# Another order for the seven products of a pooled pair, collected in one PSUM tile with ScalarE copies between

## The chip, the core and the metric

The kernel runs on one core of one Trainium2 chip. The metric is the device time of one execution in microseconds (us). Before the change the median of three runs is 782.64 us (782.56 to 784.69).

## What is computed

The reference is a small decoder trunk with two layers, 512 tokens (16 meta tokens are put in front of them and dropped at the end) and a width of 1024. All values are fp32. In each layer one normalised input is projected by one wide matrix, and two token mixers work side by side on slices of the result; each mixer's output is gated by a sigmoid of a slice of its own.

```
h = rmsnorm(h_res, norm_gain[l])
proj = h @ w_in[l]
u_pool, z_pool, c_q, c_kv, k_rope, z_mla, g_pool, g_mla = jnp.split(proj, IN_SPLIT_POINTS, axis=-1)
y_pool = (pool_mix(u_pool, pool_w_group[l], pool_scale[l]) * jax.nn.silu(z_pool)) @ pool_w_up[l]
o_mla = mla(c_q, c_kv, k_rope, pos, ...)
y_mla = (o_mla * jax.nn.silu(z_mla)) @ mla_w_up[l]
merged = jax.nn.sigmoid(g_pool) * y_pool + jax.nn.sigmoid(g_mla) * y_mla
h_res = h_res + merged @ w_out[l]
```

The change concerns only one matrix product: g_pool = h @ (its 1024 columns of w_in), in the last layer.

## The kernel before

**Products in three matmuls.** Activations lie with channels on the 128 partitions and tokens along the free axis. Every fp32 operand is split into a rounded high part and a low part, and a product is the sum of three matmuls, high x high, low x high and high x low (`mm3`, L192, L195, L196). Weights come in chunks of 128 x 512: SP's queue loads a chunk into one of three buffers raw (L115), ScalarE casts it to whi (L187), VectorE subtracts to get wlo (L188); whi and wlo have three buffers each. Chunks are loaded a few products ahead.

**The order of the work.** A list `plan` names the products (a Gemm each) in the order of the program, and the generator `stream()` issues it piece by piece. In the last layer the plan's end runs gm0, gm1, gp0, gm2, gp1, gm3, gp2, gm4, gp3, gm5, gm6, gm7: gm are the tiles of the other gate, gp0 to gp3 the four pairs of g_pool's eight tiles. Attention runs beside it: each head is issued in steps, and between two steps `fill` advances the stream by a fixed number of nanoseconds as the generator counts them. A scheduler in the framework then sets the final order of each engine's instructions; so the order that is run differs in places from the one that is written. The engines PE (TensorE), ACT (ScalarE), DVE (VectorE), POOL (GpSimd) and SP (SyncE, which only issues DMAs) each run their instructions in that order and wait on semaphores.

**Seven products for eight.** In the last layer a pair of g_pool's tiles (256 output channels) is worked out by a Strassen-Winograd scheme: two halves of the input channels (chunks 0 to 3 and 4 to 7 of h) and two halves of the tokens (256 each) make it a 2 x 2 block product, done in seven products in place of eight. Products 1, 2 and 3 take plain tokens; 4, 5, 6 and 7 take sums and differences of token halves that `mixed` (L588) prepares on VectorE as the input is normalised. The sums of weight blocks for 3, 5, 6 and 7 are made in DRAM by accumulating DMAs early on (wsumgp). A product is 12 matmuls of 128 x 256 (four input chunks, three matmuls each). Its result goes to a PSUM tile called mm, of which there are four, shared with all other Gemms.

`fast` (L608 to 654) issues the pair u in the order 1, 6, 7, 5, 2, 4, 3 with four PSUM tiles: a holds 1, onto which 2 is accumulated; b holds 6; c holds 7, onto which 4 is accumulated; d holds 5, onto which 3 is accumulated. After 1, ScalarE copies a to part[u] in SBUF (a slot of the tag sv, L632). VectorE subtracts 6 from it (L634), subtracts that from 7 (L636) and 5 from the result (L638), which is one of the four blocks; 2 lets a second block be read straight from PSUM; after 4 VectorE subtracts (L644), and after 3 it adds (L647). Each finished block goes to `got_gp` (L655): a tanh on ScalarE (L657) and one VectorE operation (L658) that multiplies it into the pooled mixer's output am.

**What stands beside it.** In the stretch of the pairs TensorE also runs the other gate's tiles (mm<-hh,whi, 512 columns), the scores of a head (S<-kh,qhl), transposes of its probabilities (L979, written mm<-cst,pa and mm<-cst,cq), its output (o<-th,vt, L984) and transposes at L990 and L1007. ScalarE casts (th, L303) and takes exponentials (L915). SP's queue also moves rotated keys: kp<-kn (L866) and, when that has landed, kn<-kp (L877), ahead of whatever was queued later. In the output stage behind the gates, a PSUM tile S is emptied by ScalarE (sv<-S, L1163) and used again for the next products; it is named here because the prediction reads some of its rows.

Of the kernel before, what the change touches and what calls it, by code (L numbers as in the profile page):

```python
# [13 lines left out]
AF = mybir.ActivationFunctionType  # L14
# [4 lines left out]
P = 128  # L19
# [3 lines left out]
NM = 16  # L23
T = SEQ + NM
HALF = T // 2
# [14 lines left out]
MT_GP = 16  # L40
# [32 lines left out]
def trunk(ctx, tc, xT, pos, win, wkr, wqb, wkb, wvb, wgr, wpu, wmu, wout, gains, const, yT):  # L73
    nc = tc.nc
    pe, act, dve, gp, sp = nc.tensor, nc.scalar, nc.vector, nc.gpsimd, nc.sync
# [115 lines left out]
    def mm3(out, wh, wl, xh, xl, start, stop, more=False, hold=False):  # L191
        first = pe.matmul(out, wh, xh, start=start, stop=False, skip_group_check=more)  # L192
        if hold:
            behind(first, newest[0])
        pe.matmul(out, wh, xl, start=False, stop=False, skip_group_check=more)  # L195
        newest[0] = pe.matmul(out, wl, xh, start=False, stop=stop, skip_group_check=more)  # L196
        past.append((clk[0], newest[0]))
# [140 lines left out]
    wsum = {n: [dp.tile([P, 4, 512], F32, name=f"wsum{n}{u}") for u in range(k)] for n, k in (("gp", 4), (0, 2), (1, 2))}  # L338
    gate = dp.tile([P, 6, SEQ], F32, name="gate")
# [3 lines left out]
    N2 = SEQ // 2  # L343
    XH = [(NM, NM + N2), (NM + N2, T)]
    (a, b), (_, c) = XH

    def weight_sums(name, w):
# [13 lines left out]
        for u in range(len(w) // 2):  # L361
            for fn, i in ((copy, 0), (copy, 2), (add, 0), (copy, 1), (add, 2), (add, 1), (copy, 3), (add, 3)):
                yield lambda fn=fn, u=u, i=i: fn(*made(u, i))

    class Layer:
        def __init__(self, l):
            self.l, self.last = l, l == DEPTH - 1
# [218 lines left out]
        def mixed(self, i):  # L586
            k, s = divmod(i, 2)
            if k > 3 or not self.last:  # L588
                return
            u, w = self.f[k], self.f[k + 4]  # L590
            if s == 0:
                dve.tensor_sub(w[:, b:c], u[:, b:c], w[:, b:c])
                dve.tensor_sub(u[:, b:c], u[:, a:b], u[:, b:c])
                dve.tensor_sub(u[:, a:b], u[:, a:b], w[:, b:c])
                dve.tensor_sub(w[:, a:b], w[:, a:b], u[:, a:b])
                return
            if k == 0:
# [10 lines left out]
        def fast(self, name, a, b, u, got):  # L608
            order = (1, 6, 7, 5, 2, 4, 3)
            s = wsum["gp"][u]  # L610
            src = {1: a[:, 0:512], 2: a[:, 512:1024], 4: b[:, 512:1024], 5: s[:, 0, :], 6: s[:, 1, :], 7: s[:, 2, :],
                   3: s[:, 3, :]}
            bank = {}

            def body(i, w):
                p = order[i]
                key = {1: "a", 2: "a", 6: "b", 7: "c", 4: "c", 5: "d", 3: "d"}[p]
                if key not in bank:
                    bank[key] = mmt()
                ps = bank[key][:, :N2]  # L620
                t, o = (XH[1] if p == 3 else XH[0]), (0 if p == 1 else 4)
                for k in range(4):
                    xh, xl = (x[:, t[0]:t[1]] for x in self.hs[k + o]) if p < 4 else self.tt[k][p]
                    c = P * k
                    mm3(ps, w[0][:, c:c + P], w[1][:, c:c + P], xh, xl, k == 0 and p not in (2, 4, 3), k == 3, True)
                    if k == 1:
                        yield 6 * (N2 / 2.4)
                if p == 1:
                    self.part[u] = slot("sv", bufs=2)
                d, v = self.part[u][:, 0:N2], self.part[u][:, HALF:HALF + N2]  # L630
                if p == 1:
                    act.activation(d, ps, AF.Copy)  # L632
                elif p == 6:
                    dve.tensor_sub(d, d, ps)  # L634
                elif p == 7:
                    dve.tensor_sub(v, ps, d)  # L636
                elif p == 5:
                    dve.tensor_sub(v, v, ps)  # L638
                    got(2 * u + 1, XH[1], v, v)
                elif p == 2:  # L640
                    got(2 * u, XH[0], ps, tmp()[:, :N2])
                elif p == 4:
                    x = tmp()[:, :N2]
                    dve.tensor_sub(x, ps, d)  # L644
                    got(2 * u + 1, XH[0], x, x)
                else:
                    dve.tensor_add(d, d, ps)  # L647
                    got(2 * u, XH[1], d, d)
                if i == len(order) - 1:
                    done.add((self.l, name))  # L650
                yield 6 * (N2 / 2.4)

            plan.append(Gemm((self.l, name), [src[p] for p in order], 512 * len(order), body=body))

        def got_gp(self, m, s, v, t):  # L655
            am = self.am[m][:, s[0]:s[1]]
            act.activation(t, v, AF.Tanh, scale=0.5)  # L657
            dve.scalar_tensor_tensor(out=am, in0=t, scalar=1.0, in1=am, op0=ALU.add, op1=ALU.mult)  # L658

        def window(self, m):  # L660
            s = self.us[m]
# [551 lines left out]
        def register(self, nxt):  # L1213
            l, XS = self.l, self.XS
            wi = lambda t: win[l, t]
# [49 lines left out]
            if self.last:  # L1265
                for e in ("gm0", "gm1", "gp0", "gm2", "gp1", "gm3", "gp2", "gm4", "gp3", "gm5", "gm6", "gm7"):
                    m = int(e[2])
                    if e[:2] == "gp":
                        self.fast(e, wi(MT_GP + 2 * m), wi(MT_GP + 2 * m + 1), m, self.got_gp)
# [179 lines left out]
```

## Time and profile before

| what | value |
|---|---|
| runs | 782.64 us median (782.56 to 784.69) |
| the profiled execution | 782.78 us; its span 781.0 us |
| TensorE, matmuls | 774.8 us busy, 99% of the span, 5469 instructions |
| VectorE | 568.6 us, 73% |
| ScalarE | 445.2 us, 57% |
| GpSimd | 233.3 us, 30% |
| the four pairs | from about 608 to 692 us after the span's start |

The span is the time from the first to the last instruction that the profiler recorded. Line numbers such as L187 are those of the kernel before. A row of the timeline gives start, duration, engine, line, operation, and the tile written and the tiles read, with buffer numbers left out; in square brackets stand the idle time of the engine ahead of the instruction and what ended it. Matmuls are pipelined: a row's duration overlaps the next row, so what a matmul costs is the distance between two starts.

### The profile page before, as it was taken

To read this page: it belongs to the slowest core of one execution; us is meant where nothing else is said; L and a number is where in the kernel's file an instruction comes from. 1 tells how busy PE (TensorE), PEld (TensorE's weight loads), DVE (VectorE), ACT (ScalarE), POOL (GpSimd) and SP (SyncE) were. 2 spreads that over 40 slices of the span, in tenths; PEclk is the share of its full clock that TensorE was granted. 3 is DMA by queue.
4 is the path that set the end of the run, shared out by engine and by line. 5 is a ranking of instruction groups with operands and counts; after the bars stand their busy time and mean duration, and the time that the engine had idled before them with its cause. 6 is when DMAs were issued, how large, how long until landed. Compare 5 with 4: busy or idle time off the path is not lost.

```text
span 781.0 us, 15326 instructions
## 1 busy us (share of the span) xinstructions
PE 774.8 (99%) x5469; PEld 712.5 (91%) x5469; DVE 568.6 (73%) x1326; ACT 445.2 (57%) x1016; POOL 233.3 (30%) x303
## 2 busy tenths in 40 slices
PE   9999999999999999999999999999999999999998
PEld 9999899999999999999997898887788999988887
DVE  5848787446778876589764477865897888864984
ACT  7645555645566665645564356546667766664462
POOL 1024525103335333211330136221006625440213
PEclk9999999999999999999999999999999999999999
DMA  6242467765746465565662524425556666662655
GB/s 244 82 97 89 124 170 151 179 167 144 156 109 165 115 141 120 155 168 175 168 170 81 98 87 123 132 63 181 141 140 162 174 174 166 176 221 75 209 154 138
DMA packets 65325, 112.92 MB, mean 145 GB/s; under 512 B 10704, under 2 KB 15696, under 8 KB 65248
## 3 DMA queue, kind: packets, MB, share of 16 engines
q1 hardware_dynamic: 55344, 92.18, 40.0%
q0 software_dynamic: 8896, 17.92, 13.0%
q10 hardware_dynamic: 1008, 1.84, 0.6%
q8 instruction: 43, 0.70, 0.4%
q14 instruction: 34, 0.28, 0.1%
HBM read 100.18 MB, written 22.62 MB: 157 GB/s over the span
## 4 chain that ended last, share of the span: by engine, by line
PE 92%; DVE 3%; DMA 2%; ACT 1%; issue 1%; SPq 0%; DVEq 0%; ACTq 0%
PE mm L192 26%; PE mm L196 26%; PE mm L195 26%; PE S L192 3%; PE S L196 2%; PE S L195 2%; PE mm L979 2%; PE o L985 1%; PE o L984 1%; DVE wlo L188 1%; PE S L506 1%; DMA raw<-win 1%; PE mm L408 1%; DMA raw<-wsum 1%; PE mm L465 0%
## 5 line engine op out<-in xcount | busy, mean ns | idle before, releaser
L192 PE MATMUL mm<-hh,whi 128*128 128x264 f32 (+2 forms) x992 | 307.0, 312 | 0.1
L196 PE MATMUL mm<-hh,wlo 128*128 128x264 f32 (+2 forms) x992 | 304.7, 309 | 0.3 <-DVE wlo L188 0.2
L195 PE MATMUL mm<-hl,whi 128*128 128x264 f32 (+2 forms) x992 | 304.4, 308 | 0.0
L188 DVE TENSOR_TENSOR wlo<-raw,whi 128x512 fp32r<-128x512 f32 (+1 forms) x253 | 179.8, 714 | 103.7 <-ACT whi L187 101.2
L187 ACT ACTIVATE whi<-raw 128x512 fp32r<-128x512 f32 (+1 forms) x253 | 154.2, 612 | 166.4 <-PE mm L195 105.0
L192 PEld LDWEIGHTS mm<-hh,whi 128*128 128x128 f32 x992 | 186.6, 189 | 11.0 <-ACT racc L993 0.5
L195 PEld LDWEIGHTS mm<-hl,whi 128*128 128x128 f32 x992 | 187.2, 189 | 8.7
L196 PEld LDWEIGHTS mm<-hh,wlo 128*128 128x128 f32 x992 | 186.2, 188 | 9.4 <-DVE wlo L188 1.1
L922 POOL TENSOR_SCALAR pa<-pa,rs 128x272 f32<-128x272 f32 (+1 forms) x32 | 33.0, 1031 | 103.0 <-DVE rs L941 64.2
L922 POOL TENSOR_SCALAR cq<-cq,rs 128x400 f32<-128x400 f32 (+1 forms) x32 | 52.2, 1631 | 0.0
L192 PE MATMUL mm<-cq,whi 128*128 128x264 f32 (+2 forms) x140 | 43.8, 313 | 0.0
L195 PE MATMUL mm<-cq,whi 128*128 128x264 f32 (+2 forms) x140 | 43.7, 312 | 0.0
L196 PE MATMUL mm<-cq,wlo 128*128 128x264 f32 (+2 forms) x140 | 43.3, 312 | 0.1
L908 DVE CUSTOM_DVE_ANT_0 S<-S,maskw,nqs 128x272 f32<-128x272 f32 (+4 forms) x80 | 38.6, 497 | 5.2 <-PE S L196 4.9
L725 POOL TENSOR_TENSOR racc<-racc,tmp 128x264 f32<-128x264 f32 (+1 forms) x15 | 14.5, 964 | 84.9 <-ACT tmp L724 84.8
L304 DVE TENSOR_TENSOR tl<-mm,th 128x512 fp32r<-128x512 f32 (+1 forms) x64 | 30.0, 482 | 8.0 <-ACT th L303 6.3
L359 POOL DMA_DIRECT2D wsum<-wout x8 | 7.0, 873 | 91.7 <-PE mm L196 77.0
L303 ACT ACTIVATE th<-mm 128x512 fp32r<-128x512 f32 (+1 forms) x64 | 26.2, 432 | 10.2 <-PE mm L979 9.6
L915 ACT ACTIVATE cq<-S,bia 128x400 f32<-128x400 f32 (+2 forms) x48 | 24.4, 513 | 13.2 <-DVE bia L953 8.5
L192 PE MATMUL mm<-u,whi 128*128 128x264 f32 (+1 forms) x96 | 31.3, 326 | 0.0
L196 PE MATMUL mm<-u,wlo 128*128 128x264 f32 (+1 forms) x96 | 30.9, 322 | 0.0
L195 PE MATMUL mm<-kn,whi 128*128 128x264 f32 (+1 forms) x96 | 30.6, 320 | 0.0
(344 smaller groups left out, 1684.2 us busy)
## 6 DMA issues: line engine op xcount, KB each, us to landing
raw<-win SPq DMA_DIRECT2D x139, 256.0 KB, 2.9
raw<-wout SPq DMA_DIRECT2D x22, 256.0 KB, 3.5
bc<-kdr SPq DMA_DIRECT2D x16, 264.0 KB, 4.6
wsum<-wout SPq DMA_DIRECT2D x16, 256.0 KB, 3.5
raw<-wpu SPq DMA_DIRECT2D x16, 256.0 KB, 3.2
wsumgp<-win SPq DMA_DIRECT2D x16, 256.0 KB, 3.3
raw<-wmu SPq DMA_DIRECT2D x16, 256.0 KB, 2.8
raw<-wsumgp SPq DMA_DIRECT2D x16, 256.0 KB, 3.6
```

The costliest lines, as they stand in the source:

```text
L187: act.activation(hi[:, :n], raw[:, :n], AF.Copy)
L188: dve.tensor_sub(lo[:, :n], raw[:, :n], hi[:, :n].bitcast(F32))
L192: first = pe.matmul(out, wh, xh, start=start, stop=False, skip_group_check=more)
L195: pe.matmul(out, wh, xl, start=False, stop=False, skip_group_check=more)
L196: newest[0] = pe.matmul(out, wl, xh, start=False, stop=stop, skip_group_check=more)
L303: act.activation(hi[:, a:b], src, AF.Copy)
L304: dve.tensor_sub(lo[:, a:b], src, hi[:, a:b].bitcast(F32))
L725: self.acc_last = gp.tensor_add(self.acc[:, a:b], self.acc[:, a:b], t[:, :b - a])
L908: dve.tensor_tensor_reduce(out=sv, in0=sv, in1=mask, scale=nqs[:, i, h:h + 1], scalar=3e38, op0=ALU.add, op1=ALU.min, accum_out=bia[:, c:c ...
L915: act.activation(pv, sv, AF.Exp, scale=-1.0, bias=bia[:, i:i + 1], accum_out=rs[:, c:c + 1])
L922: gp.tensor_scalar(pt[i], pt[i], rs[:, i:i + 1], None, op0=ALU.mult)
L979: pe.transpose(tr[:, P * (i - j):P * (i - j + 1)], pt[i][:, NM + P * j:NM + P * (j + 1)], ident)
```

## The change

The products of a pair come in the order 1, 2, 6, 7, 5, 4, 3 and take three PSUM tiles: 2 has one to itself (e), 7 and 4 share c as before, and 1, 6, 5, 3 are all accumulated one onto the other in a. Only 1, 2 and 7 start a tile afresh. ScalarE copies a away after 1 and after 6, and c after 7 (`keep`), into two slots of the tag sv, halves of which are named by kept. VectorE adds the copy of 1 to 2, subtracts 5's state of a from the copy of 7, and the copy of 6 from 4's state of c; after 3, the tanh reads a in PSUM. So a pair has three copies in place of one on ScalarE, and three operations in place of five on VectorE ahead of `got_gp`. In `mixed` a difference of tokens is taken with the other sign, so that 6 can be added to 1 and need not be subtracted. `fast` takes its weights by a kind and a first tile in place of two blocks, which are the same blocks. A helper `wi_` and a method `got_gm` come in; the latter is not called. The lines below `wi_` move by 3 and those below `fast` by more: L187 to L196 are the same in both kernels, the transposes' L979 is now L990, o's L984 is L995 (L985 is L996), the casts' L303 stays, L866 is L877 and L877 is L888, and got_gp's L657 is L661.

```diff
         def mixed(self, i):
...
                 dve.tensor_sub(w[:, b:c], u[:, b:c], w[:, b:c])
                 dve.tensor_sub(u[:, b:c], u[:, a:b], u[:, b:c])
-                dve.tensor_sub(u[:, a:b], u[:, a:b], w[:, b:c])
-                dve.tensor_sub(w[:, a:b], w[:, a:b], u[:, a:b])
+                dve.tensor_sub(u[:, a:b], w[:, b:c], u[:, a:b])
+                dve.tensor_add(w[:, a:b], w[:, a:b], u[:, a:b])
...
-            order = (1, 6, 7, 5, 2, 4, 3)
+            order = (1, 2, 6, 7, 5, 4, 3)
...
+            def keep(p, ps):
+                t = kept[p] = self.carry[p == 7][:, HALF * (p == 6):HALF * (p == 6) + N2]
+                act.activation(t, ps, AF.Copy)
...
-                key = {1: "a", 2: "a", 6: "b", 7: "c", 4: "c", 5: "d", 3: "d"}[p]
+                key = {2: "e", 7: "c", 4: "c"}.get(p, "a")
...
-                    mm3(ps, w[0][:, c:c + P], w[1][:, c:c + P], xh, xl, k == 0 and p not in (2, 4, 3), k == 3, True)
+                    mm3(ps, w[0][:, c:c + P], w[1][:, c:c + P], xh, xl, k == 0 and p in (1, 2, 7), k == 3, True)
...
                 if p == 1:
-                    self.part[u] = slot("sv", bufs=2)
-                d, v = self.part[u][:, 0:N2], self.part[u][:, HALF:HALF + N2]
-                if p == 1:
-                    act.activation(d, ps, AF.Copy)
-                elif p == 6:
-                    dve.tensor_sub(d, d, ps)
-                elif p == 7:
-                    dve.tensor_sub(v, ps, d)
+                    self.carry = [slot("sv", bufs=2) for _ in range(2)]
+                if p in (1, 6, 7):
+                    keep(p, ps)
+                elif p == 2:
+                    t = tmp()[:, :N2]
+                    dve.tensor_add(t, ps, kept[1])
+                    got(2 * u, XH[0], t, t)
                 elif p == 5:
-                    dve.tensor_sub(v, v, ps)
-                    got(2 * u + 1, XH[1], v, v)
-                elif p == 2:
-                    got(2 * u, XH[0], ps, tmp()[:, :N2])
+                    t = self.carry[1][:, HALF:HALF + N2]
+                    dve.tensor_sub(t, kept[7], ps)
+                    got(2 * u + 1, XH[1], t, t)
                 elif p == 4:
-                    x = tmp()[:, :N2]
-                    dve.tensor_sub(x, ps, d)
-                    got(2 * u + 1, XH[0], x, x)
+                    t = tmp()[:, :N2]
+                    dve.tensor_sub(t, ps, kept[6])
+                    got(2 * u + 1, XH[0], t, t)
                 else:
-                    dve.tensor_add(d, d, ps)
-                    got(2 * u, XH[1], d, d)
+                    got(2 * u, XH[1], ps, tmp()[:, :N2])
```

The numbers of instructions are 5261 on PE in both, 938 for 930 on ACT, 1302 for 1310 on DVE. Three places of the order are shown, all in the second pair (gp1).

TensorE of the changed kernel, around the end of product 7. Tile mm_8632 is c; the first two rows are the last two matmuls of 7, and 4 begins where whi_8648, its weights, is first read; mm_8736 belongs to the next Gemm, a tile of the other gate, whose chunk is whi_8710:

```order
L195 MATMUL mm_8632<-sq_7778,whi_8575 128x256
L196 MATMUL mm_8632<-sq_7777,wlo_8576 128x256
L996 MATMUL o_8593<-tl_8614,vt 128x384
L192 MATMUL mm_8736<-hh_6_132,whi_8710 128x512
L195 MATMUL mm_8736<-hl_7_133,whi_8710 128x512
L990 MATMUL mm_8756<-cst,cq_1575_8281 128x128
L990 MATMUL mm_8756<-cst,cq_1576_8282 128x128
L192 MATMUL mm_8632<-sq_7767,whi_8648 128x256
L195 MATMUL mm_8632<-sq_7768,whi_8648 128x256
L196 MATMUL mm_8632<-sq_7767,wlo_8649 128x256
```

TensorE of the kernel before, behind the end of product 7, whose last matmul is the first row (c is mm_8574 there):

```order
L196 MATMUL mm_8574<-sq_7777,wlo_8551 128x256
L979 MATMUL mm_8594<-cst,pa_8277 128x128 x2
L979 MATMUL mm_8594<-cst,cq_1574_8278 128x128
L979 MATMUL mm_8594<-cst,cq_1575_8279 128x128
L195 MATMUL S_8665<-kl_8463,qhl_105 128x288
L196 MATMUL S_8665<-kh_8462,qhl_106 128x288
L192 MATMUL S_8665<-kh_8462,qhl_105 128x144
L195 MATMUL S_8665<-kl_8463,qhl_105 128x144
L196 MATMUL S_8665<-kh_8462,qhl_106 128x144
L979 MATMUL mm_8605<-cst,pa_8277 128x128
```

In before eleven rows of attention and the twelve matmuls of 2 stand between 7 and 4; in the changed kernel one row of attention (o), two matmuls of the next Gemm and two transposes, and the next Gemm's first matmul is the second instruction behind 7.

ScalarE of the changed kernel: whi_8628 is the chunk of 5, whi_8648 that of 4; sv_8520<-mm_8507 is the copy of a after 6, and tmp_8569 the tanh of 2:

```order
L187 ACTIVATE whi_8628<-raw_8626 128x512
L926 ACTIVATE pa_8523,rs_8527<-S_8529,bia_8526 128x272
L985 ACTIVATE pmr_8594<-pmr_8594 128x4x32
L661 ACTIVATE tmp_8569<-tmp_8569 128x256
L187 ACTIVATE whi_8648<-raw_8646 128x512
L620 ACTIVATE sv_8520<-mm_8507 128x256
L303 ACTIVATE th_8603<-mm_8598 128x512
```

And a few rows on, with the copy of c after 7 behind the casts for 3 and for the next Gemm:

```order
L187 ACTIVATE whi_8688<-raw_8686 128x512
L187 ACTIVATE whi_8710<-raw_8708 128x512
L620 ACTIVATE sv_8521<-mm_8632 128x256
L303 ACTIVATE th_8759<-mm_8756 128x256
L661 ACTIVATE sv_8521<-sv_8521 128x256
```

ScalarE of the kernel before, where sv_8519<-mm_8506 is the copy after 1, whi_8624 the chunk of 2 and whi_8646 that of 4:

```order
L187 ACTIVATE whi_8570<-raw_8568 128x512
L632 ACTIVATE sv_8519<-mm_8506 128x256
L999 ACTIVATE tmp_8487<-o_8353 64x512
L915 ACTIVATE cq_1627_8522,rs_8525<-S_8536,bia_8524 128x400
L187 ACTIVATE whi_8624<-raw_8622 128x512
L915 ACTIVATE pa_8521,rs_8525<-S_8527,bia_8524 128x272
L187 ACTIVATE whi_8646<-raw_8644 128x512
L303 ACTIVATE th_8599<-mm_8594 128x512
```

Before's one copy stands behind the cast of 5's chunk (whi_8570); in the changed kernel the copy of 6 stands directly behind the cast of 4's chunk, and that of 7 behind the casts for 3 and for the next Gemm.

SP's queue of the changed kernel (wsumgp holds the sums of weights for 7, 5 and 3 in this order here, win the plain weights, raw_8646 those of 4):

```order
L874 DMA bc_8744<-kdr_122 128x528
L877 DMA kp_6464<-kn_1206_6712 64x528
L115 DMA raw_8573<-wsumgp_124 128x512
L115 DMA raw_8626<-wsumgp_124 128x512
L888 DMA kn_1206_6712<-kp_6464 64x528
L115 DMA raw_8646<-win 128x512
L115 DMA raw_8686<-wsumgp_124 128x512
```

SP's queue of the kernel before (wsumgp for 5; win for 2 and then for 4):

```order
L863 DMA bc_8742<-kdr_122 128x528
L866 DMA kp_6464<-kn_1206_6712 64x528
L115 DMA raw_8568<-wsumgp_124 128x512
L877 DMA kn_1206_6712<-kp_6464 64x528
L115 DMA raw_8622<-win 128x512
L115 DMA raw_8644<-win 128x512
L115 DMA raw_8684<-wsumgp_124 128x512
```

The load of 5's chunk comes ahead of kn<-kp in both; in before the loads for 2 and 4 stand behind it, in the changed kernel that for 4 alone, with a load for 3 next.

More of the change, by code (lines that the diff above doesn't have):

```diff
@@ L363, in weight_sums, with wi_ @@
                 yield lambda fn=fn, u=u, i=i: fn(*made(u, i))
+    def wi_(l, t):
+        return win[l, t]
     class Layer:
@@ L606, in mixed, with fast @@
             self.tt[k] = {6: (th[:, a:b], tl[:, a:b]), 5: (th[:, b:c], tl[:, b:c]), 7: (t3h, t3l), 4: (t4h, t4l)}
-        def fast(self, name, a, b, u, got):
-            order = (1, 6, 7, 5, 2, 4, 3)
-            s = wsum["gp"][u]
+        def fast(self, name, wt, kind, u, got):
+            order = (1, 2, 6, 7, 5, 4, 3)
+            a, b, s = wi_(self.l, wt + 2 * u), wi_(self.l, wt + 2 * u + 1), wsum[kind][u]
             src = {1: a[:, 0:512], 2: a[:, 512:1024], 4: b[:, 512:1024], 5: s[:, 0, :], 6: s[:, 1, :], 7: s[:, 2, :],
                    3: s[:, 3, :]}
-            bank = {}
+            bank, kept = {}, {}
+            def keep(p, ps):
+                t = kept[p] = self.carry[p == 7][:, HALF * (p == 6):HALF * (p == 6) + N2]
+                act.activation(t, ps, AF.Copy)
             def body(i, w):
                 p = order[i]
-                key = {1: "a", 2: "a", 6: "b", 7: "c", 4: "c", 5: "d", 3: "d"}[p]
+                key = {2: "e", 7: "c", 4: "c"}.get(p, "a")
                 if key not in bank:
@@ L658, in got_gp, with got_gm @@
             dve.scalar_tensor_tensor(out=am, in0=t, scalar=1.0, in1=am, op0=ALU.add, op1=ALU.mult)
+        def got_gm(self, m, s, v, t):
+            if self.gms[m] is None:
+                self.gms[m] = slot("ts" if m % 2 else "tc")
+            d = self.gms[m][:, s[0]:s[1]]
+            act.activation(d, v, AF.Tanh, scale=0.5)
+            act.dma_start(gate[:, m, s[0] - NM:s[1] - NM], d)
         def window(self, m):
@@ L1268, in register @@
                     if e[:2] == "gp":
-                        self.fast(e, wi(MT_GP + 2 * m), wi(MT_GP + 2 * m + 1), m, self.got_gp)
+                        self.fast(e, MT_GP, "gp", m, self.got_gp)
                     else:
```

## The prediction

> **What bounds the kernel now.** The page comes first: the busy shares of the engines, and the shares of the chain of work that ended last.
>
> ```profile
> span 781.0 us, 15326 instructions
> PE 774.8 (99%) x5469; PEld 712.5 (91%) x5469; DVE 568.6 (73%) x1326; ACT 445.2 (57%) x1016; POOL 233.3 (30%) x303
> PE 92%; DVE 3%; DMA 2%; ACT 1%; issue 1%; SPq 0%; DVEq 0%; ACTq 0%
> ```
>
> TensorE is busy for 774.8 of 781.0 us and makes up 92% of the chain. The change leaves the matmuls as they are in number and shape (five products of a pair were accumulated onto others before, and are now laid onto other partners), so its effect can only come through the 6.2 us in which TensorE is not busy: what it adds to them or takes from them. The second view is the busy time by windows, for the stretch that holds the four pairs and for the second pair alone; the third is the list of waits of TensorE in the stretch 590 to 690.
>
> ```profile
> core 0: us, PE busy (x) PEld busy (x) DVE busy (x) ACT busy (x) POOL busy (x), PEclk, DMA share, GB/s
> 608.00:700.00 92.00, 91.66 (x639) 84.59 (x639) 78.72 (x198) 62.93 (x162) 42.34 (x49) 1.00 0.68 185
> 630.00:655.00 25.00, 24.70 (x175) 22.70 (x174) 19.48 (x51) 15.94 (x42) 10.22 (x11) 1.00 0.62 152
> ```
> ```profile
> PE mm L196 <- DVE wlo L188: 0.2, 1, 0.2
> ```
>
> In 92 us TensorE misses 0.34, at a granted clock of 1.00, and one single wait is listed. ScalarE is busy for 62.93 of 92.00 us (68%), VectorE for 78.72 (86%), so neither is a bound by its sum; what counts is whether a result is ready when TensorE's fixed order gets to it. The profiled execution lasted 782.78 us (span 781.0 and 1.8 around it), 0.02% above the median of 782.64, so sums made on its rows stand for the median. A measurement of this kernel can tell about 0.3% from no change, which is 2.35 us: below 780.3 is faster, above 785.0 slower.
>
> **The change part by part.** First the work of the engines. The copies of before and VectorE's operations on a product are grouped by line, with minimum, median and maximum in ns; the cast of one weight chunk and the landing of the raw chunks come from the same view of other tiles.
>
> ```profile
> L632 ACT ACTIVATE sv<-mm x4: 365/380/387, 611.7 to 678.4; 128x256 f32<-128x256 f32 x4
> L636 DVE TENSOR_TENSOR sv<-mm,sv x4: 404/418/425, 617.5 to 683.0; 128x256 f32<-128x256 f32 x4
> ```
> ```profile
> L187 ACT ACTIVATE whi<-raw x75: 615/632/639, 560.3 to 767.9; 128x512 fp32r<-128x512 f32 x75
> ...
> DMA to landing us min/median/max: 2.5/3.2/6.3
> ```
>
> Each pair gets two more copies on ScalarE: 8 x 0.38 = 3.0 us in 92, which makes it busy for 66 us (72%). VectorE loses two operations of a pair, 8 x 0.418 = 3.3 us, and falls to 75 us (82%). The negated difference only swaps operands and turns one subtraction into an addition of the same shape. None of it lies on TensorE's path by its sum: **0 us**, and the cover is the 29 us in which ScalarE is idle in this stretch.
>
> Second, **the new waits**. Products 1, 6, 5 and 3 now share one PSUM tile, so 6 may not start before ScalarE has copied 1 away, 5 not before 6 is copied, 3 not before VectorE has read 5; and 4 not before 7 is copied. Four waits a pair, 16 in all. Before has three a pair (2 behind the copy of 1, 4 and 3 behind VectorE's reading of 7 and 5), with whole products between, and the list of waits above shows none of them. The nearest rows with thin cover are in the output stage, where one PSUM tile is emptied by ScalarE in between and TensorE goes on in it. The timeline shows two hand-overs there, the first with TensorE's rows around it, the second with the copy too; times are start and duration.
>
> ```profile
> 756.93 0.28 PE L195 MATMUL mm<-sq,whi 128*128 128x256 f32 x1
> ...
> 757.47 0.39 PE L192 MATMUL S<-cq,whi 128*128 128x256 f32 x1 [0.26 <-ACT sv L1163]
> 757.69 0.28 PE L195 MATMUL S<-u,whi 128*128 128x256 f32 x1
> ```
> ```profile
> 762.66 0.28 PE L196 MATMUL S<-cq,wlo 128*128 128x256 f32 x1
> ...
> 762.98 0.38 ACT L1163 ACTIVATE sv<-S 128x256 f32<-128x256 f32 x1 [0.39 <-PE S L196]
> ...
> 763.41 0.39 PE L192 MATMUL S<-cq,whi 128*128 128x256 f32 x1 [0.23 <-ACT sv L1163]
> ```
> ```profile
> L1163 ACT ACTIVATE sv<-S x12: 363/372/383, 379.6 to 770.5; 128x264 f32<-128x264 f32 x6, 128x256 f32<-128x256 f32 x6
> ...
>   PE S L192: 0.5, 2
> ```
>
> From the start of the last matmul of the old content to the start of the first of the new one are 763.41 - 762.66 = 0.75 us. A matmul of this shape takes 0.12 from start to start (1.29 us for the eleven steps between the first two rows below), so 0.63 us of other matmuls cover a hand-over wholly. Where cover lacks, as at 756.93, the step takes 0.54 in place of 0.12 and the next one 0.22 (757.69 - 757.47) in place of 0.12: 0.42 + 0.10 = **0.52 us** for a hand-over with one matmul between. Only 2 of the 12 such copies were waited for.
>
> What covers the 16 waits is read from the changed order with durations from these rows of TensorE: one product, matmuls of 512 columns, a row of seven transposes in the chain, and four 96-row transposes.
>
> ```profile
> 610.47 0.28 PE L192 MATMUL mm<-cq,whi 128*128 128x256 f32 x1
> ...
> 611.76 0.28 PE L196 MATMUL mm<-cq,wlo 128*128 128x256 f32 x1
> ```
> ```profile
> 604.00 0.39 PE L192 MATMUL mm<-hh,whi 128*128 128x512 f32 x1
> 604.23 0.40 PE L195 MATMUL mm<-hl,whi 128*128 128x512 f32 x1
> ```
> ```profile
> 623.00 0.76 PE mm L979 x7
> ```
> ```profile
> 641.88 0.48 PE L990 MATMUL mm<-identr,pmr 128*96 128x128 f32 x4
> 642.19 0.33 PE L192 MATMUL mm<-cq,whi 128*128 128x256 f32 x1
> ```
>
> So a product is 12 x 0.117 = 1.41 us, 512 columns 0.23, a transpose 0.76 / 7 = 0.11, four of the other kind 0.31. Where a whole product or more lies between, as the written order has it for 1 to 6, 5 to 3 and 7 to 4, the cover is above 1.4 against 0.63. The scheduler has narrowed two of them. In the second pair, between 7 and 4 lie one matmul of 384 columns (0.17 by the share of columns), two of 512 and two transposes: 0.17 + 0.46 + 0.22 = 0.85 us, 0.22 to spare. In the third pair, 6 comes right behind 1 with 1.15 us of attention and transposes between, 0.52 to spare. Taken alone, all 16 waits are covered: **0 us**, with bounds of 0 and 16 x 0.52 = 8.3 us.
>
> The Trainium skill, page "PSUM — Partial Sum Buffer", section "Summary: rules for kernel authors", says to read PSUM in a different bank from the one that a running matmul writes, and to guard with semaphores by bank. This change puts reader and writer of four products into one bank. By that rule every hand-over would be a stop, 8.3 us as priced from the rows above; the row with 2 waits for 12 copies speaks for a price of 0 where enough other matmuls lie between.
>
> Third, **one place that the order exposes by itself**. In the second pair the next gate's first matmul now stands right behind product 7 (its chunk is whi_8710 in the rows on the change), and the cast of that chunk goes into the buffer that 7's eleventh matmul is the last to read. From that matmul's start s: end s + 0.28 (the duration in its row), hand-over and cast 0.04 + 0.63, hand-over to TensorE 0.05: s + 1.00. TensorE is there at s + 2 x 0.12 + 0.17 = s + 0.41. So 0.59 us are idle and 0.10 go with the restart: **+0.7 us**. In before the pair's second product and eleven other instructions stood at this place. The copy of 7 stands behind the cast, ready at s + 0.95 + 0.38 + 0.05 = s + 1.38; TensorE reaches 4 at s + 1.10 + 0.68 = s + 1.78, so that one stays covered.
>
> Fourth, **the late load in the second pair**. The chain, ScalarE's and TensorE's timelines, and the waits of SP's queue:
>
> ```profile
> 631.35 5.68 DMA raw<-win
> ```
> ```profile
> 637.12 0.63 ACT L187 ACTIVATE whi<-raw 128x512 fp32r<-128x512 f32 x1 [1.28 <-DMA raw<-win]
> ...
> 638.12 0.62 ACT L187 ACTIVATE whi<-raw 128x512 fp32r<-128x512 f32 x1
> ```
> ```profile
> 637.53 0.38 PE L979 MATMUL mm<-cst,cq 128*128 128x128 f32 x2
> 637.80 0.39 PE L192 MATMUL mm<-hh,whi 128*128 128x256 f32 x1
> 638.02 0.28 PE L195 MATMUL mm<-hl,whi 128*128 128x256 f32 x1
> 638.53 0.39 PE L196 MATMUL mm<-hh,wlo 128*128 128x256 f32 x1 [0.22 <-DVE wlo L188]
> ...
> 644.35 0.49 PE L979 MATMUL mm<-cst,cq 128*128 128x128 f32 x3
> 644.91 0.50 PE L196 MATMUL mm<-hh,wlo 128*128 128x512 f32 x1
> ```
> ```profile
> SPq L115 <- DVE wlo L188: 19.7, 14, 4.0
> SPq L877 <- DMA kp<-kn: 7.0, 2, 3.9
> ```
>
> In before the load of product 2's weights is queued on SP behind kn<-kp, which waits for kp to land; it is issued at 631.35, takes 5.68 us, and 2 starts at 637.80 when its cast is done, then waits for wlo: 0.51 - 0.12 = 0.39 at 638.02, with 0.10 of restart and about 0.1 ahead of 637.80, **0.6 us** that leave, since the chunk of the product now in this place, 5, is loaded ahead of kn<-kp. What is late next: 4's chunk is now the first behind kn<-kp, its cast stands in ScalarE's queue directly ahead of the copy of 6, and 5 waits for that copy. TensorE has done the same amount of work by then: 637.53 + about 0.14 + 0.31 for four transposes moved here = 637.98. If the cast starts as the first cast did (637.12), the copy ends at 637.12 + 0.63 + 0.38 = 638.13 and 5 starts at 638.18, 0.2 late; if as the second did, at 638.12, 1.2 late. Before's rows have nothing nearer; I take the middle, **+0.7 us**, which replaces what left. Queued behind the waiting cast are also two casts th of the attention, which TensorE needs only behind 5, 1.41 us later. The short stall at 644.35 (0.56 less three transposes of 0.11 = 0.23, with restart 0.3) is left as it is: its cause, a cast and its wlo behind VectorE's queue, is there after the change too.
>
> The sum: 782.8 + 0.7 + 0.7 - 0.6 = **783.6 us**.
>
> **The rivals.** *A small gain.* Eight fewer operations on VectorE bring wlo forward, the place behind 7 is covered, the copy of 6 is at its early end, and both stalls of before go: 782.8 - 0.6 - 0.3 + 0.2 = 782.1. For it speaks that both stalls end with VectorE; against it that the cast behind 7 is released by TensorE itself.
>
> *Slower by ScalarE's queue.* ScalarE works in order, and a copy that TensorE waits for now stands behind a cast that waits for a load. In before a late load delayed only its own product; now it also delays one whose weights are long there. The load's buffer comes free with a wlo of VectorE, and the longest such wait of SP is 4.0 us. Issued that much later, 5 in the second pair starts 4.0 us later: 787.6. Every microsecond beyond the forecast's landing counts in full, and 1.4 us decide for slower. For it speak the spread of landings, 2.5 to 6.3 us, and the same arrangement in the third pair (0.52 to spare ahead of 6); against it that 4's load follows a buffer whose wlo is early.
>
> *Slower by every hand-over.* All 16 waits are exposed like the one at 756.93, because operations queue ahead of the copies all over: 782.8 + 8.3 = 791.1. Against it: 2 of 12.
>
> *The change doesn't do what it says.* The scheduler puts 5 ahead of 7 in the second pair and 6 ahead of 2 in the third, so the written distances don't hold there. That is in the forecast already; it gives no time of its own.
>
> **How the numbers follow.** Forecast 0.48 (0.46 of it within 0.3%), small gain 0.13 (0.03 of it faster by over 0.3%, for that needs more than the stalls found here), ScalarE's queue 0.30 (0.27 slower), every hand-over 0.09. Faster 0.03, same 0.46 + 0.10 + 0.03 = 0.59, slower 0.02 + 0.27 + 0.09 = 0.38. The range goes from 781.5 (half a microsecond below the small gain) to 788.0 (the queue's case and a little): left out are the hand-overs, 0.09, and ends of the other two, about 0.1.
>
> **What would show it.** In the profile after: a TensorE wait for whi at the next gate's first matmul behind 7 of the second pair, about 0.6 us; no wait for wlo at the third matmul of 2; a wait of 5 for sv of 0.2 to 1.2; no waits for sv elsewhere. 16 PSUM reads by copies and VectorE of about 0.4 us, and TensorE busy for 774.8 again. The prediction is wrong if TensorE waits for sv at most of the 16 places, or if the loads land otherwise around 637, or if stalls come up behind the pairs, where the scheduler has also shifted instructions and I found no reason for any.

## The result, and the profile after

The changed kernel took 784.98 us (median of 14 runs, 783.6 to 787.76), the kernel before 782.94 us (14 runs). The ratio is 1.0029 with a 95% interval of 1.0019 to 1.0039: 2.0 to 2.3 us slower, at the edge of the 0.3% that the prediction took as the bound between no change and slower. The forecast was 783.6, its range 781.5 to 788.0.

First the page of the changed kernel, then its busy time by windows:

```profile
span 782.8 us, 15305 instructions
PE 773.7 (99%) x5469; PEld 710.8 (91%) x5469; DVE 566.8 (72%) x1318; ACT 448.0 (57%) x1024; POOL 228.8 (29%) x303
```
```profile
608.00:700.00 92.00, 89.03 (x620) 81.69 (x619) 74.89 (x187) 63.56 (x166) 35.23 (x46) 1.00 0.64 177
630.00:655.00 25.00, 23.05 (x163) 20.99 (x161) 18.17 (x44) 15.77 (x40) 10.78 (x15) 1.00 0.64 171
```

ScalarE has 2.8 us more to do, where 3.0 were worked out, and VectorE 1.8 us less, where 3.3 were. In the stretch of the pairs TensorE now misses 2.97 of 92 us, where it missed 0.34. The span tells of less (1.8 us), because this execution happened to start faster: a matmul in front of the attention that comes at the same place in both orders starts at 532.71 in before and at 531.56 here. From there to the end it is 248.3 us before and 251.2 after. One profiled execution carries about 1 us of such chance, so what a variant costs is taken from the medians, and the profiles only say where.

The waits of TensorE in the stretch 590 to 690 (us in total, times, longest), which were a single one of 0.2 us before:

```profile
PE o L996 <- DVE tl L304: 0.8, 2, 0.6
PE mm L1001 <- DVE wlo L188: 0.7, 1, 0.7
PE mm L192 <- ACT sv L620: 0.5, 1, 0.5
PE mm L192 <- ACT whi L187: 0.4, 1, 0.4
PE mm L990 <- DVE tmp L1021: 0.2, 1, 0.2
PE mm L192 <- DVE tmp L1021: 0.2, 1, 0.2
```

One of the 16 new hand-overs is in it (sv L620). The others are work of the attention and casts. They lie in two places and a remainder. The timeline of TensorE, first pair, then second pair:

```profile
620.50 0.28 PE L196 MATMUL mm<-rinv,wlo 128*128 128x256 f32 x1
621.03 0.33 PE L990 MATMUL mm<-cst,pa 128*128 128x128 f32 x1 [0.25 <-DVE tmp L1021]
...
621.33 0.47 PE L995 MATMUL o<-th,vt 128*128 128x512 f32 x1
622.36 0.50 PE L996 MATMUL o<-tl,vt 128*128 128x512 f32 x1 [0.55 <-DVE tl L304]
...
637.72 0.27 PE L196 MATMUL S<-kh,qhl 128*128 128x144 f32 x1
638.72 0.55 PE L1001 MATMUL mm<-identr,pmr 128*96 128x128 f32 x4 [0.73 <-DVE wlo L188]
639.82 0.39 PE L192 MATMUL mm<-cq,whi 128*128 128x256 f32 x1 [0.54 <-ACT sv L620]
...
643.94 0.34 PE L996 MATMUL o<-tl,vt 128*128 128x384 f32 x1
644.70 0.50 PE L192 MATMUL mm<-hh,whi 128*128 128x512 f32 x1 [0.43 <-ACT whi L187]
645.04 0.39 PE L195 MATMUL mm<-hl,whi 128*128 128x512 f32 x1
```

Distance from start to start, less what the first matmul takes: 0.41 and 0.80 us in the first pair; in the second 0.93 ahead of the four transposes of pmr, 0.79 ahead of product 5 (639.82 - 638.72 - 0.31), 0.59 behind product 7. The two of the first pair, and the transposes', were in no term of the prediction.

**Where the first pair's waits come from.** SP's queue, the landing time of that one load (asked for 608 to 611), and the casts of ScalarE and VectorE:

```profile
609.36 0.54 SPq L115 DMA_DIRECT2D raw<-win  x1
```
```profile
raw<-win SPq DMA_DIRECT2D x1, 256.0 KB, 6.6
```
```profile
616.02 0.63 ACT L187 ACTIVATE whi<-raw 128x512 fp32r<-128x512 f32 x1 [3.29 <-PE o L996]
616.56 0.37 ACT L620 ACTIVATE sv<-mm 128x256 f32<-128x256 f32 x1
```
```profile
616.69 0.69 DVE L188 TENSOR_TENSOR wlo<-raw,whi 128x512 fp32r<-128x512 f32 x1 [3.46 <-PE mm L196]
617.30 0.50 DVE L919 CUSTOM_DVE_ANT_0 S<-S,maskw,nqs 128x272 f32<-128x272 f32 x1
```

The chunk of product 4 is issued at 609.36 and lands 6.6 us later, at 615.96; its cast starts at 616.02. The releaser in the brackets had long been done: the wait was for the landing. Until then ScalarE stood idle for 3.29 us and VectorE for 3.46 us, each with other work queued behind this chunk (on VectorE the masking of the scores, on ScalarE the copy of 6 and then work of the attention). Product 4 itself was not late. The attention was, five microseconds on. In before a load issued at the same point (609 to 612) was as late, but its cast stood behind the attention's work in both queues, and nobody waited. The landing time, and ScalarE's row of the cast, which has no idle time ahead of it:

```profile
raw<-win SPq DMA_DIRECT2D x1, 256.0 KB, 6.1
```
```profile
617.55 0.63 ACT L187 ACTIVATE whi<-raw 128x512 fp32r<-128x512 f32 x1
```

**The second pair's** start with a late chunk as well, that of 7; the chain of work that ended last has it, and ScalarE's timeline the transposes' pmr at the end of it:

```profile
629.30 4.73 DMA raw<-wsumgp
634.12 0.64 ACT whi L187
634.78 0.69 DVE wlo L188
635.47 0.42 DVE S L919
```
```profile
638.37 0.30 ACT L985 ACTIVATE pmr<-pmr 128x128 fp32r<-128x128 f32 x1
...
638.88 0.62 ACT L187 ACTIVATE whi<-raw 128x512 fp32r<-128x512 f32 x1
639.40 0.37 ACT L620 ACTIVATE sv<-mm 128x256 f32<-128x256 f32 x1
```

The scores' masking on VectorE waits behind the cast of 7's chunk, the exponentials on ScalarE behind the masking, and pmr ends at 638.67, 0.05 ahead of the transposes (the wlo in their row's brackets is not what they read). The copy of 6 stands behind the cast of 4's chunk, as forecast, but this cast is late by the queue and no longer by its load, which was issued at 634.33 and landed 4.0 us later, 0.5 ahead of the cast.

### The profile page after: what moved, and what is told of

Same layout as the page of the kernel before. It is cut to its first block, busy times and chain, and to the rows that moved or that the text cites. A ratio compares the mean times of both kernels' runs of the same rounds, so it can differ in the third digit from the quotient of the medians.

```text
span 782.8 us, 15305 instructions
## 1 busy us (share of the span) xinstructions
PE 773.7 (99%) x5469; PEld 710.8 (91%) x5469; DVE 566.8 (72%) x1318; ACT 448.0 (57%) x1024; POOL 228.8 (29%) x303
## 4 chain that ended last, share of the span: by engine, by line
PE 90%; DVE 4%; DMA 2%; ACT 1%; issue 1%; SPq 0%; ACTq 0%; DVEq 0%
PE mm L192 26%; PE mm L196 25%; PE mm L195 25%; PE S L195 2%; PE S L192 2%; PE S L196 2%; PE mm L990 2%; DVE wlo L188 1%; PE o L996 1%; PE o L995 1%; PE S L509 1%; ACT whi L187 1%; DMA raw<-wsumgp 1%; PE mm L411 1%; DVE S L919 1%
## 5 line engine op out<-in xcount | busy, mean ns | idle before, releaser
L196 PE MATMUL mm<-hh,wlo 128*128 128x264 f32 (+2 forms) x992 | 304.5, 309 | 0.0
L187 ACT ACTIVATE whi<-raw 128x512 fp32r<-128x512 f32 (+1 forms) x253 | 154.3, 613 | 170.4 <-PE mm L195 108.9
L196 PEld LDWEIGHTS mm<-hh,wlo 128*128 128x128 f32 x992 | 185.8, 188 | 8.6 <-DVE wlo L188 0.3
L933 POOL TENSOR_SCALAR cq<-cq,rs 128x400 f32<-128x400 f32 (+1 forms) x32 | 50.4, 1575 | 0.0
L196 PE MATMUL mm<-cq,wlo 128*128 128x264 f32 (+2 forms) x140 | 43.4, 312 | 0.1
L919 DVE CUSTOM_DVE_ANT_0 S<-S,maskw,nqs 128x288 f32<-128x288 f32 (+4 forms) x80 | 38.4, 497 | 4.7 <-PE S L196 4.5
L303 ACT ACTIVATE th<-mm 128x512 fp32r<-128x512 f32 (+1 forms) x64 | 26.3, 435 | 10.6 <-PE mm L990 10.3
L196 PE MATMUL mm<-u,wlo 128*128 128x264 f32 (+1 forms) x96 | 30.9, 322 | 0.0
```

The source lines that it names most:

```text
L187: act.activation(hi[:, :n], raw[:, :n], AF.Copy)
L303: act.activation(hi[:, a:b], src, AF.Copy)
L919: dve.tensor_tensor_reduce(out=sv, in0=sv, in1=mask, scale=nqs[:, i, h:h + 1], scalar=3e38, op0=ALU.add, op1=ALU.min, accum_out=bia[:, c:c ...
L933: gp.tensor_scalar(pt[i], pt[i], rs[:, i:i + 1], None, op0=ALU.mult)
```

## The experiments

Two theories were set against each other. **L**: weight chunks that land late stand at the head of ScalarE's and VectorE's queues in the order that the scheduler makes, and what is behind them comes late. **B**: the hand-overs in a shared PSUM tile cost by themselves. A third, **O** (the new order is bad whatever the loads do), came up after the first runs. Each kernel was timed in five rounds beside the kernel before on the same chip; before's median there was 782.95 us for the first four kernels, 781.98 for the next four and 781.92 for the last four, so kernels of different groups are compared by their ratios.

### The parts apart

The new order alone, with the tiles, the copy and the sums of before:

```diff
-            order = (1, 6, 7, 5, 2, 4, 3)
+            order = (1, 2, 6, 7, 5, 4, 3)
```

> The kernel before with the new order of products alone (1, 2, 6, 7, 5, 4, 3), its four PSUM tiles, its one copy and its VectorE sums kept. Theory L (late weight chunks at the head of ScalarE's and VectorE's queues, as the new order of loads and casts puts them) expects about as much loss as the change has, 784 to 786 us. Theory B (the hand-overs in one shared PSUM tile) expects none, 782.9 us, since this kernel has only the three waits a pair of before.

Measured: 787.72 us, ratio 1.0064 (1.0044 to 1.0084), 4.8 us slower. The tile that 1, 6, 5 and 3 share in the changed kernel can't be the cause of that, and the order alone costs more than twice what the whole change costs. Without hand-overs this kernel is not: in the new order 2 is written directly behind 1, onto whose tile a it is accumulated, and in the second pair it waited for the copy of 1:

```profile
638.77 0.39 PE L192 MATMUL mm<-hh,whi 128*128 128x256 f32 x1 [1.08 <-ACT sv L632]
```

That copy stood in ScalarE's queue behind a cast for whose chunk ScalarE had waited 3.65 us, so the row shows theory L's mechanism at a hand-over. It is 1.1 of the 4.8 us.

The other part, the changed kernel with the old order:

```diff
-            order = (1, 2, 6, 7, 5, 4, 3)
+            order = (1, 6, 7, 5, 2, 4, 3)
```

> The changed kernel with the old order of products (1, 6, 7, 5, 2, 4, 3): the shared tile, the three copies and the negated difference stay. Theory B expects the whole loss or more, 785 to 787 us, because 6 follows 1 more closely. Theory L expects the time of before, 782.5 to 784 us, unless a late chunk stands at the head of a queue in this order too.

Measured: 785.37 us, ratio 1.0033 (1.002 to 1.0045). As theory B has it by the number, but not by the waits of TensorE in 590 to 690:

```profile
PE mm L192 <- ACT th L303: 1.3, 1, 1.3
PE mm L196 <- DVE wlo L188: 1.0, 1, 1.0
PE mm L192 <- ACT whi L187: 0.6, 1, 0.6
PE o L996 <- DVE tl L304: 0.4, 1, 0.4
PE mm L990 <- POOL pa L933: 0.3, 1, 0.3
```

No product waits for a copy (sv) there; the waits end with casts and with work of the attention. That speaks against theory B. It doesn't show theory L either: ahead of the longest wait, at 623 us, ScalarE had waited for a landing for 0.2 us only, and what made that cast late was not followed further. So the parts don't add up (4.8 and 2.4 against 2.0): each makes the scheduler put the instructions of these 90 us into another order, and each order has its own waits.

### Taking the late load away

What makes the load of 609.36 land late is seen in SP's queue: at 608.75 it issued a copy for the output stage's weight sums (wsum<-wout, 6.2 us to landing), and GpSimd adds to another at the time. The sums can be made earlier; the order of TensorE's instructions hardly moves by it (49 rows of the difference in the changed kernel, 2 in before).

```diff
                 for i, fn in enumerate(weight_sums(1, [wout[1, m] for m in OUT])):
-                    after(4500 * (i + 1), fn)
+                    after(2000 * (i + 1), fn)
```

> The changed kernel with the weight sums for the output stage (DMAs that copy and accumulate in DRAM) issued every 2.0 us and not every 4.5 us of the stream's count, so that they are over before the pairs begin; nothing else is edited. Theory L expects weight chunks to land sooner in the first two pairs and 1 to 2 us to come back, 783 to 784 us. Theory B expects no difference from the changed kernel, 785.0 us.

Measured: 783.82 us, ratio 1.0016 (1.0006 to 1.0026): 1.1 us of the 2.0 came back, though the two intervals overlap; what is clear is where the waits went. The waits of TensorE in 590 to 690 and the landing times of weight chunks in 600 to 645 (this line is 2.6/3.6/6.6 for the changed kernel):

```profile
PE mm L990 <- POOL pa L933: 1.0, 1, 1.0
PE mm L192 <- ACT whi L187: 0.4, 1, 0.4
PE mm L192 <- DVE tmp L1021: 0.2, 1, 0.2
```
```profile
DMA to landing us min/median/max: 2.5/3.3/4.2
```

No chunk lands later than 4.2 us, and all waits at 621, 622, 638 and 639 us are gone, the one for the copy of 6 included. The cast behind 7 is left, and one wait for GpSimd at 593 us is new.

The control, before with the same edit:

> The kernel before with the same earlier weight sums, as a control. Theory L expects its two stalls behind late chunks (0.6 and 0.3 us) to shrink, 782 to 782.9 us; theory B expects 782.9 us.

Measured: 783.19 us, ratio 1.0002 (0.9993 to 1.0011). Its stalls behind 637 went too, and the wait for GpSimd at 593 us came in their place:

```profile
PE mm L979 <- POOL pa L922: 1.3, 1, 1.3
PE S L192 <- ACT kh L303: 0.2, 1, 0.2
```

One chunk still took 6.3 us in this control: it was asked for at 600.01 us, beside an add of the sums that GpSimd had issued at 599.67. Between the two kernels with early sums there is 0.6 us, which their intervals don't separate; the exposed cast was priced at 0.7.

### Sums out of the stretch, and the cast's own buffer

To be rid of the wait at 593, the sums were issued from the start of the layer (far), a hundred us ahead of the pairs. The lines that issued them later go. In the second edit the gate tile behind the second pair casts its chunks into another pool:

```diff
+            if l == 1:
+                for i, fn in enumerate(weight_sums(1, [wout[1, m] for m in OUT])):
+                    after(6000 * (i + 1), fn)
             up("ckv1")
```
```diff
                         add(e, wi(MT_GM + m), D, evac=self.ev_gate(m), xs=hs, segs=XS)
+                        plan[-1].spare = e == "gm3"
```

> The kernel before with the output stage's weight sums issued from the start of the last layer, every 6.0 us of the stream's count, far ahead of the pairs; nothing else is edited. In the stretch of the first two pairs the DMAs of the sums are gone. Theory L (late weight chunks at the head of ScalarE's and VectorE's queues) expects the two stalls of before (0.6 and 0.3 us) to go and GpSimd's stall of the other early placing not to come: 782.0 us. If the loads were late for another reason, 782.9 us.

> The changed kernel with the same far placing of the weight sums. Theory L expects only the exposed cast behind product 7 of the second pair (0.7 us) to be left of the change's cost: 0.7 us above the kernel before with the far sums, 782.7 to 783.5 us. Theory B (hand-overs in the shared tile) expects the whole 2 us to stay, 785.0 us.

> The changed kernel with the far sums, and the chunks of the gate tile behind the second pair cast into buffers of another pool, so that their first cast need not wait for product 7. The stall of 0.58 us and its restart behind product 7 should go: 0.5 to 0.7 us below the same kernel without this edit, 782.0 to 783.0 us. If the scheduler's other shifts eat it, no difference.

Measured: 782.98 (ratio 1.0011, 1.0002 to 1.002), 783.88 (1.0023, 1.0013 to 1.0033) and 783.71 us (1.0017, 1.0007 to 1.0026). In the stretch it went as theory L has it: no wait over 0.2 us in before, the cast behind 7 (0.4) and one at 659 (0.2) in the changed kernel, none of either with the own buffer. In total it did not. Before lost 1.0 us: with this placing it has waits of 0.7 us each at 453 and 463 us, at the layer's start, where it had none. The own buffer's gain of 0.2 us is within its interval. And with the own buffer 0.7 us were left above before with the same placing (783.71 against 782.98), with no stall in the stretch to account for them; their intervals overlap, and where they went is open.

So a third placing (mid): every 5.0 us from the end of the key factors on, behind 463 us and mostly ahead of 593. The lines that issued them later go here too.

```diff
             self.k_factors()
+            if l == 1:
+                for i, fn in enumerate(weight_sums(1, [wout[1, m] for m in OUT])):
+                    after(5000 * (i + 1), fn)
```

> The kernel before with the output stage's weight sums issued earlier by some 60 us, every 5.0 us of the stream's count from the end of the key factors of the last layer on: behind the place where the far placing cost 1 to 2 us (waits at 447 to 463 us), and mostly ahead of the place where the early placing cost 1.3 us (GpSimd at 593 us). If late chunks are what the sums do to the pairs, the 0.9 us of stalls behind 637 go and nothing comes: 781.5 to 782.3 us where before has 782.5. If every placing costs as much as it saves, no difference.

> The changed kernel with the same placing of the weight sums. Theory L expects the exposed cast behind product 7 of the second pair (0.7 us) and the wait at 659 us (0.4 and a restart) to be left: 0.7 to 1.2 us above the kernel before with this placing. Theory B (hand-overs) expects 2 us above it.

> As change_sums_mid, and the chunks of the gate tile behind the second pair in buffers of another pool. Theory L expects both stalls that were left to go and the time of the kernel before with this placing, within 0.5 us; theory B expects no gain, since the 16 hand-overs are all there.

Measured: 783.30 (1.0017, 1.0009 to 1.0026), 784.36 (1.0029, 1.0019 to 1.004) and 783.23 us (1.0019, 1.0009 to 1.0029). The waits of TensorE in 590 to 690 of the changed kernel, then of the one with its own buffer; before has none there:

```profile
PE mm L192 <- ACT whi L187: 0.4, 1, 0.4
PE mm L192 <- DVE tmp L1021: 0.2, 1, 0.2
```
```profile
PE o L996 <- DVE tl L304: 0.2, 1, 0.2
```

With this placing the change costs 1.06 us, and with the cast's own buffer nothing (783.23 against 783.30), though all 16 hand-overs are there. The two intervals leave room for about 1 us of difference, not for 2: theory B is out as the cause of the change's cost. As a whole the placing cost before 1.4 us: a wait of 1.2 to 1.3 us for a cast (whi) came at 541 us in all kernels of this placing. Each of the three other placings took waits away here and made one elsewhere; none of the versions beat the kernel before.

### A hand-over without cover

The changed kernel, mid placing, with the gate tile's first matmul held behind product 4, so that 0.17 us lie between 7 and 4:

```diff
-                            xs[k][0][:, a:b], xs[k][1][:, a:b], k == 0, k == K - 1)
+                            xs[k][0][:, a:b], xs[k][1][:, a:b], k == 0, k == K - 1,
+                            hold=k == 0 and g_.name == (1, "gm3"))
```

> As change_sums_mid, but the first matmul of the gate tile behind the second pair is held behind product 4, so that only one matmul of 384 columns is left between 7 and 4 (0.17 us where a hand-over needs 0.63). Theory B, the price of a hand-over by itself: 4 waits 0.46 us and 0.10 go with the restart. Theory L: the copy of 7 still stands behind the cast of the gate tile's chunk, which waits for 7's eleventh matmul, so 4 starts at 1.38 us from that matmul's start where TensorE is there at 0.41: a wait of 1.0 us, and 0.10 with the restart.

Measured: 784.01 us, ratio 1.0027 (1.0015 to 1.0038), not to be told from the kernel without the hold: the wait of 0.6 for the cast behind 7 is gone, a wait of product 4 for the copy of 7 has come in its place, and another product waits 0.5 for a wlo at 665 us. TensorE and ScalarE at the hand-over:

```profile
643.40 0.28 PE L195 MATMUL mm<-sq,whi 128*128 128x256 f32 x1
643.52 0.28 PE L196 MATMUL mm<-sq,wlo 128*128 128x256 f32 x1
643.64 0.34 PE L997 MATMUL o<-tl,vt 128*128 128x384 f32 x1
644.67 0.39 PE L192 MATMUL mm<-sq,whi 128*128 128x256 f32 x1 [0.70 <-ACT sv L621]
```
```profile
643.72 0.63 ACT L187 ACTIVATE whi<-raw 128x512 fp32r<-128x512 f32 x1
644.25 0.37 ACT L621 ACTIVATE sv<-mm 128x256 f32<-128x256 f32 x1
```

4 starts 644.67 - 643.64 - 0.17 = 0.86 us late; 0.46 of it is the hand-over's own as worked out ahead (0.63 - 0.17), and the rest is the cast ahead of the copy in ScalarE's queue. Theory L said 1.0. The cast started 0.32 after the eleventh matmul (643.72 - 643.40), as worked out, and the copy began ahead of its end by 0.1.

### The order by itself

The first experiment again, with the sums far:

> The kernel before with the new order of products alone, and the far placing of the weight sums. Without the far placing this order cost 4.8 us. Theory L expects most of it back, 783 to 785 us. Theory O (the order that the scheduler makes of it is bad by itself, whatever the loads do) expects about 787 us again.

Measured: 788.55 us, ratio 1.0077 (1.0063 to 1.0091), 6.6 us slower, with no chunk later than 4.5 us. Theory L's forecast (783 to 785) fails here, and moving the sums brought nothing back; the time is nearer to what theory O expects (about 787). The longest wait, 2.8 us, is that of transposes for ScalarE, which was busy from 636.8 almost without a break until it had made their input, as VectorE nearly was. A lower clock behind that wait adds 1.7 us (last section), and three waits at 709 to 718 us, behind the pairs, add 1.4. What of the loss is the dense order and what the chunk whose landing ScalarE had awaited at 632.7 (2.2 us) was not taken apart and stays open.

## Why the prediction was right, and where it was off

The time lies in the range, and the four signs that were named came: the wait for whi behind 7, the wait of 5 for sv, no wait for wlo in 2, no other wait for sv. So the mechanism was there as described, but it was not the whole: the terms that were left out or mis-sized below come to 2.6 us in the profile (1.2 + 1.0 + 0.4), and that the time still lies in the range owes something to the range's width, which was taken up to 788.0 for the rival "ScalarE's queue".

- **The work** (0 us): right. ScalarE took 2.8 us more, and lost nothing by it.
- **The 16 hand-overs** (0 us): right, by the kernels with moved sums, where none is waited for (the held one apart, which was made to lay one bare) and, with the cast's own buffer and the mid placing, the time is that of before. The spare time worked out for the closest two held: 7 to 4 in the second pair is not waited for, nor 1 to 6 in the third. With 0.17 us of cover a hand-over comes to 0.46 us by the rows, and in the held kernel product 4 came 0.86 late. The Trainium skill ("PSUM — Partial Sum Buffer", "Summary: rules for kernel authors") says to read another bank than the one that a running matmul writes, and to guard by bank with semaphores. The guard is what these kernels have, and it showed no price of its own where other matmuls lie between; reading a bank while it is written was tried in no run here.
- **The cast behind product 7** (0.59 and 0.10): right in place and size: 0.59 in the profile after, and 0.11 with the restart (645.04 - 644.70 = 0.34 where 0.23 is usual). Giving the cast its own buffer took 1.1 us off in the mid placing and 0.2 in the far one, each within the spread of its runs, but in both the wait is gone from the profile.
- **The late load in the second pair** (+0.7 for 0.6 that leave): this is the term that was mis-sized. The 0.6 left as forecast (no wait for wlo at product 2), and 5 did wait for the copy of 6, 0.79 us. But the step counted only 5 as late behind ScalarE's queue and looked, of the other work queued there, at two casts alone, which are needed later. The four transposes ahead of 5 needed pmr, which stands in the same queue behind a chunk that landed 4.73 us after its issue, and waited 0.93. Together it is 1.7 us in place of 0.7, and 0.4 more a little later.
- **What was left out**: the first pair, 1.2 us. The prediction looked for late loads where before had stalls, and so at the second pair alone. The load of 609.36 was as late in before (6.1 us) and left no mark, because its cast stood behind the work of the attention and not ahead of it. The trace had the landing; the new order showed what had come to stand behind it. The rival "ScalarE's queue" named this mechanism, with the second and third pair as its places; it came about in the first and second, on VectorE's queue as much as on ScalarE's.
- **The small gain** did not come: the stalls of before did go, the one at 644.35 too, which the forecast had left in place, and larger ones came.

## What to carry to other kernels

Where a change lets a scheduler reorder a stretch, look up every transfer in it that lands late in the old trace, also those for which nobody waited, and read in the new order what stands behind its first user on each in-order engine. Price that, and not the user. A transfer's lateness has a cause in another queue, and moving that cause away is an experiment that leaves the order nearly as it is; here it told a queue's cost from a PSUM tile's, which taking the change apart did not.

## What the runs showed of the hardware

A chunk of 256 KB asked for between 600 and 645 us landed in 2.4 to 4.7 us in the eight kernels whose weight sums were placed far or mid, and in up to 6.6 us beside the sums (6.3 in before).

A long wait of TensorE cost more than itself; one profiled execution shows it. In the kernel with the new order and far sums, TensorE could have gone on at 638.8 and did at 641.76; the granted clock (the column behind POOL's) then was 0.57 on the mean of 4 us, 0.50 from 643 to 645 us, and a matmul of 256 columns took 0.21 where it takes 0.12:

```profile
642.00:646.00 4.00, 4.00 (x21) 3.81 (x21) 2.61 (x5) 1.67 (x4) 3.35 (x7) 0.57 0.24 73
646.00:650.00 4.00, 4.00 (x36) 4.00 (x35) 2.47 (x7) 1.94 (x4) 0.00 (x0) 1.00 0.32 90
```
```profile
642.73 0.41 PE L192 MATMUL mm<-sq,whi 128*128 128x256 f32 x1
642.94 0.41 PE L195 MATMUL mm<-sq,whi 128*128 128x256 f32 x1
```

That is 4.0 x (1 - 0.57) = 1.7 us on top of a wait of 3.0 us; the wait of 1.5 us in the kernel with the new order alone lowered nothing. The Trainium skill, "TensorE: Matmul & The Clock Gate", Part 1, says that the clock falls to half after an idle window of about 3.4 us and comes back after a busy one. The half clock is what the trace has; the wait before it was shorter than that window, 3.0 us.
